# Up projection: high and low parts side by side in one tile, multiplied by the high weights in one matmul of 512 columns

## The chip, the cores and the metric

The kernel runs on one core of one Trainium2 chip. The metric is the device time of one execution in microseconds; the time before is the median of three runs.

The core has five engines, each with an instruction queue of its own that is worked off in order: PE (TensorE, matmuls; its weight loads are listed apart as PEld), DVE (VectorE), ACT (ScalarE), POOL (GpSimd) and SP (SyncE, which here only issues DMAs). They meet only at semaphores.

## The reference

One transformer block over 512 latent tokens (T) of width 2048, with a context prefix of 256 tokens, all in float32. The change is in the feed-forward part:

```python
def conv_ffn(h, w_up, cw, cb, w_down):
    u = dwconv3(h @ w_up, cw, cb)
    a, g = jnp.split(u, 2, axis=-1)
    return (a * jax.nn.silu(g)) @ w_down

# in reference(), after attention, short convolution and the output projection:
hf_l = modulate(rms_norm(x, g_ffn_norm[l]), sh_f, sc_f)
x = x + gt_f * conv_ffn(hf_l, w_up[l], ffn_conv_w[l], ffn_conv_b[l], w_down[l])
```

`h` is 512 x 2048, `w_up` is 2048 x 11008 (twice 5504: a and g), `dwconv3` a convolution of width 3 along the tokens.

## The kernel before, in words

Everything is held transposed: features on the 128 partitions, the 512 tokens along the columns. The feed-forward width of 5504 is 43 tiles of 128 (index f), each with an a part and a g part; the 2048 input features are 16 tiles (k or j).

**Float32 as two parts.** A matmul here reads operands of the type float32r. To keep float32 accuracy, every operand is split into a high part (an ACT cast to float32r) and a low part (DVE: the value minus the high part). A product is then three matmuls into the same PSUM bank: high weights x high values, high weights x low values, low weights x high values. That is `mm3` (lines 185 to 189), and so the matmuls of nearly the whole kernel stand at lines 187, 188 and 189. A tuple of two tiles, high and low, is passed as the operand.

**The inputs of the up projection.** `hf_tile` (line 931) norms and modulates tile j and splits it into `hf[j]`, two tiles of 128x512. `t_sums` (line 1075) makes from a pair of input tiles the sums and differences over the two token halves (H0, H1: columns 0 to 255 and 256 to 511) that the scheme below needs, and splits them as well: into the second half of `hf` of the even tile and into the tiles `TT`.

**The first six output tiles (uf).** The a and g parts of f = 0, 1, 2 are computed while the inputs are still being made: for k = 0 to 15, `row` (line 612) multiplies input tile k by six weight tiles into six PSUM banks. Rows 0 to 5 run in two halves of 256 columns, first all for H0, then all for H1; rows 6 to 15 (line 1155) run with 512 columns, so 18 matmuls each.

**The other 40 tiles of f.** From f = 3 on, a fast scheme for 2x2 block products is used: the blocks are the a and g part of the weights, the even and the odd input tiles, and the two token halves. It needs seven block products in place of eight, called p1, p2, p6, q5, p7, q4 and q3. Each (`product`, line 1165) has 8 input tiles of 128 and 256 columns, so 8 x 3 = 24 matmuls. Its weights, 128x1024, are split just ahead (`split4`, line 995: the high part by ACT, line 998, the low part by DVE, line 999; three buffers of each). Three PSUM banks, pa, pb and pc, are used per tile, one half of each; p6, p7 and q4 go on adding to what stands in pa, and q3 to pc. The outputs are taken out in between:

- after p1: ACT copies pa to u1 (`aside`, line 1174); after p2: DVE adds pb and u1 into the first half of cg (line 1212)
- after p6: ACT copies pa to u2; after p7: ACT copies pa to u3, and DVE makes the second half of ca from pc and u3 (line 1224)
- q4 and q3 run one tile later (`finish`, line 1177): ACT writes the first half of ca from pa with the sign changed (line 1180), DVE adds pc and u2 into the second half of cg (line 1182)

Then `acts` (line 1010) runs the convolution, the SiLU and the product of both on the full 512 columns; the result is kept (`plain`) or again turned into sums and differences (`pair_sums`, line 1035), split into high and low side by side in one tile, and stored to DRAM by POOL (line 1044), to be read again by the down projection.

**Weights.** `up_load` (line 1113) fetches five tiles of 128x1024 per f, a tile ahead, on the SP queue (line 1119); two of them get a second block added by an accumulating DMA on the POOL queue (line 1121), which must wait for the plain load. Nine buffers hold them.

**Order.** The program is written in the order of the calls, but most of it is ordered per engine by the compiler framework's scheduler, which simulates the engines' times. Only what goes through `keep` or `issue_after` has an order set by hand. So a changed instruction can change the order of others on its engine.

Of the kernel before, what the change touches and what calls it, by code (L numbers as in the profile page):

```python
# [10 lines left out]
F32 = mybir.dt.float32  # L11
# [61 lines left out]
def block_kernel(ctx, tc, xt, ctxt, ctxn, c, c_ctx, w_ada, small, w_in, w_inc, w_q, w_kv, w_out,  # L73
# [111 lines left out]
    def mm3(ps, w, x, first, last, on_top=False):  # L185
        with tc.issue_after(behind.pop()) if behind else ExitStack():
            PE.matmul(ps, w[0], x[0], start=first, stop=False, skip_group_check=on_top)  # L187
        PE.matmul(ps, w[0], x[1], start=False, stop=False, skip_group_check=on_top)  # L188
        PE.matmul(ps, w[1], x[0], start=False, stop=last, skip_group_check=on_top)  # L189


# [720 lines left out]
    def whole(raw, xs, nm, ps=None, cols=slice(0, T), ld=None, often=False):  # L912
# [162 lines left out]
    def t_sums(j):  # L1075

        e, o = xres[2 * j], xres[2 * j + 1]
        i, c = j // 2, HS[j % 2]
        if j % 2 == 0:
            for n in (1, 2, 4):  # L1080
                TT[n, i] = tuple(t2([P, T], F32R, f"T{n}{i}{z}") for z in "hl")

        def put(dst, src):
            hi, lo = dst
            A.copy(out=hi, in_=src)
            V.tensor_tensor(out=lo, in0=src, in1=hi.bitcast(F32), op=ALU.subtract)
# [3 lines left out]
        put(half_of(hf[2 * j], 1), e[:, H1])  # L1090
        V.scalar_tensor_tensor(out=o[:, H1], in0=e[:, H0], scalar=-1.0, in1=o[:, H1], op0=ALU.mult, op1=ALU.subtract)
        V.scalar_tensor_tensor(out=o[:, H0], in0=o[:, H1], scalar=-1.0, in1=o[:, H0], op0=ALU.mult, op1=ALU.subtract)
        for n, src in ((1, e[:, H0]), (2, o[:, H1]), (4, o[:, H0])):
            put(tuple(z[:, c] for z in TT[n, i]), src)

    def operand(n, j):
        if n in ("11", "3"):
            return half_of(hf[2 * j], n == "3")
        if n in ("21", "22"):
            return half_of(hf[2 * j + 1], n == "22")  # L1100
        return half_of(TT[int(n), j // 2], j % 2)

# [10 lines left out]
    def up_load(f):  # L1113
# [8 lines left out]
        return r  # L1122

    pss = [bank_of(i, f"uf{g}") for g, i in enumerate((2, 3, 4, 5, 1, 0))]
    held = [first_weights(k, k > 2) for k in range(EARLY)]
    for k in range(3, EARLY):
        hf_tile(k, H0)
    for k in range(EARLY):
        row(pss, held[k], hf[k], k, H0)
        pump(1)  # L1130
    drain()
    for k in range(EARLY):
        hf_tile(k, H1)
        row(pss, held[k], hf[k], k, H1)
        pump(1)
        if k in (3, 5):
            t_sums(k // 2 - 1)
# [9 lines left out]
    for k in range(EARLY, NK):  # L1147
        w = nxt
        if k + 1 < NK:
# [4 lines left out]
            nxt = prepare(k + 1)  # L1154
        row(pss, w, hf[k], k)
        if k % 2:
# [8 lines left out]
    def product(ps, a, n, nm, first):  # L1165

        w = split4(a, 1024, nm)
        for j in range(8):
            mm3(ps[:, :256], part(w, j), operand(n, j), first and j == 0, j == 7, on_top=not first)
        pump(1)  # L1170

    def aside(ps, nm):
        r = cp.tile([P, 256], F32, tag="uu", bufs=4, name=nm)
        A.copy(out=r, in_=ps[:, :256])
        return r

    def finish(st):
        f, a22, s4, u2, u3, pa, pc, cg, ca = st
        product(pa, a22, "4", f"u{f}q4", False)
        A.activation(ca[:, H0], pa[:, :256], AF.Identity, scale=-1.0)  # L1180
        product(pc, s4, "22", f"u{f}q3", False)
        V.tensor_tensor(out=cg[:, H1], in0=pc[:, :256], in1=u2, op=ALU.add)  # L1182
        acts(f, cg, ca)
# [15 lines left out]
    for f in range(G // 2, NF):  # L1199
# [7 lines left out]
        cg = cp.tile([P, T], F32, tag="cg", bufs=2, name=f"cg{f}")  # L1207
        ca = cp.tile([P, T], F32, tag="ca", bufs=2, name=f"ca{f}")
# [4 lines left out]
        V.tensor_tensor(out=a11, in0=a11, in1=s1, op=ALU.add)  # L1213
# [380 lines left out]
```

## Time and profile before

| | us |
|---|---|
| median of 3 runs (lowest, highest) | 2149.96 (2146.95, 2152.8) |
| the profiled execution: its own time | 2158.83 |
| its span, from the first to the last instruction | 2157.0 |
| mean granted TensorE clock in it | 0.994 |

The groups in the page name an instruction by line, engine and operation, then the tile written and the tiles read, the shapes and the count; behind the bar stand its busy time, the mean length in ns, and the idle time of the engine just before it with what ended it. A matmul's length in the timeline is not its price: matmuls overlap, and the distance from the start of one to the start of the next is what PE spends on it. `ufwk` are the weights of the first six tiles, `u18p6h` the high part of the weights of product p6 of f = 18, `u18a` its bank pa, `hf` and `T` the inputs. `d` and `dw` belong to the first part of the down projection, which uses 512 columns; `s`, `pq` and `pc` to attention and the projections ahead of it.

### The profile page before, as it was taken

The page shows a single profiled execution, that of the slowest core. Times are in us where ns is not written, and L with a number is a line of the kernel's source. Part 1 is how long each engine was busy: PE and PEld are TensorE (multiplying, and loading weights), DVE is VectorE, ACT ScalarE, POOL GpSimd, SP SyncE. Part 2 cuts the span into 40 slices and gives each one's busy share as a digit, 9 for nine tenths or more (in the row PEclk, how much of TensorE's full clock was granted, in tenths as well). Part 3 has the DMA queues.
Part 4 walks back from the last instruction along what each step waited for, and adds up shares of the span by engine and source line. Part 5 has one row for each costly group of instructions (what it writes and reads, how often), then busy time and mean ns, then how long its engine had stood idle before and what let it go on. Part 6 is the DMA issues. An engine that isn't in the chain of part 4 may idle for free.

```text
span 2157.0 us, 37744 instructions
## 1 busy us (share of the span) xinstructions
PE 2104.9 (98%) x14458; PEld 1946.7 (90%) x14458; DVE 1769.0 (82%) x2859; ACT 1047.1 (49%) x1710; POOL 188.1 (9%) x270
## 2 busy tenths in 40 slices
PE   7899999999999999999999999999999999999997
PEld 4688788888888888999999999999999889999997
DVE  7998987778886889788888788788888658888877
ACT  5533333555552237555555555555555333333445
POOL 0000000000000000111211111111111000000000
PEclk9999999999999999999999999999999999999998
DMA  9979785334559986577887877877887999877683
GB/s 335 345 275 337 270 279 176 128 126 162 177 199 348 344 278 192 159 217 201 241 232 215 240 229 220 237 231 219 241 229 218 341 335 290 254 220 236 196 247 111
DMA packets 162121, 513.89 MB, mean 238 GB/s; under 512 B 18962, under 2 KB 23314, under 8 KB 156306
## 3 DMA queue, kind: packets, MB, share of 16 engines
q1 hardware_dynamic: 133364, 418.14, 56.5%
q0 software_dynamic: 27488, 92.29, 18.3%
q8 instruction: 113, 1.85, 0.3%
q10 hardware_dynamic: 1088, 1.05, 0.1%
q14 instruction: 68, 0.56, 0.1%
HBM read 464.22 MB, written 46.14 MB: 237 GB/s over the span
## 4 chain that ended last, share of the span: by engine, by line
PE 86%; DVE 6%; DMA 5%; issue 1%; ACT 1%; SPq 0%; DVEq 0%; POOLq 0%; ACTq 0%
PE pp L187 4%; PE pp L189 4%; PE pp L188 4%; PE o L189 1%; PE o L187 1%; PE o L188 1%; DMA ada<-in_w_ada 1%; PE d L187 1%; PE d L189 1%; PE d L188 1%; PE uf L187 1%; PE uf L188 1%; PE of L187 1%; PE of L188 1%; PE of L189 1%
## 5 line engine op out<-in xcount | busy, mean ns | idle before, releaser
L1044 POOL DMA_DIRECT2D t_d<-tp x126 | 71.9, 574 | 468.3 <-DVE tp L1043 465.4
L255 DVE SCALAR_TENSOR_TENSOR ada<-ada,sv 128x1024 f32<-128x1024 f32 x68 | 82.1, 1219 | 12.1 <-DMA ada<-in_w_ada 12.0
L166 ACT CAST w_0h<-rw 128x512 fp32r<-128x512 f32 (+1 forms) x63 | 38.3, 618 | 108.3 <-PE pp L188 63.1
L1121 POOL DMA_DIRECT2D u_s<-in_w_up x80 | 70.2, 878 | 224.4 <-DMA u_s<-in_w_up 131.5
L233 DVE SCALAR_TENSOR_TENSOR ada<-ada,sv 128x1024 f32<-128x1024 f32 x64 | 77.5, 1217 | 4.4 <-DMA ada<-in_w_ada 3.9
L522 DVE SCALAR_TENSOR_TENSOR ada<-ada,svc 128x1024 f32<-128x1024 f32 x64 | 76.0, 1220 | 2.3 <-DMA ada<-in_w_ada 2.3
L785 POOL TENSOR_TENSOR gr<-gr,half 128x8 f32<-128x8 f32 x4 | 10.1, 2524 | 628.7 <-DVE gr L784 536.8
L1042 ACT CAST tp<-a 128x256 fp32r<-128x256 f32 x90 | 34.7, 405 | 60.5 <-DMA t_d<-tp 54.1
L167 DVE TENSOR_TENSOR w_0l<-rw,w_0h 128x512 fp32r<-128x512 f32 (+1 forms) x63 | 42.6, 681 | 22.3 <-ACT w_0h L166 22.3
L255 DVE SCALAR_TENSOR_TENSOR ra<-ra,sv 128x1024 f32<-128x1024 f32 x44 | 52.5, 1217 | 1.1 <-DMA ra<-in_w_ada 1.1
L1213 DVE TENSOR_TENSOR u<-u,u_s 128x1024 f32<-128x1024 f32 x40 | 48.8, 1219 | 0.7 <-DMA u_s<-in_w_up 0.7
L1214 DVE TENSOR_TENSOR u<-u,u 128x1024 f32<-128x1024 f32 x40 | 48.7, 1218 | 0.0
L1043 DVE TENSOR_TENSOR tp<-a,tp 128x256 fp32r<-128x256 f32 x90 | 36.2, 418 | 12.3 <-ACT tp L1042 12.3
L756 ACT CAST pth<-t 128x384 fp32r<-128x384 f32 x64 | 28.6, 485 | 26.4 <-PE t L753 26.4
L1042 ACT CAST tp<-ts 128x256 fp32r<-128x256 f32 x36 | 14.6, 407 | 43.5 <-DMA t_d<-tp 41.1
L533 DVE TENSOR_TENSOR acc<-acc,pp 128x512 f32<-128x512 f32 x50 | 34.0, 680 | 2.1 <-PE pp L189 2.1
L757 DVE TENSOR_TENSOR ptl<-t,pth 128x384 fp32r<-128x384 f32 x64 | 33.2, 549 | 2.7 <-ACT pth L756 2.7
L737 DVE TENSOR_REDUCE mn<-s 128x1 f32<-128x768 f32 x32 | 30.4, 952 | 4.8 <-PE s L726 4.6
L1043 DVE TENSOR_TENSOR tp<-ts,tp 128x256 fp32r<-128x256 f32 x36 | 15.2, 421 | 23.3 <-ACT tp L1042 23.3
L1005 ACT ACTIVATE g<-cg,sm 128x512 f32<-128x512 f32 x40 | 32.5, 813 | 0.5 <-DVE cg L1182 0.5
L1005 ACT ACTIVATE a<-ca,sm 128x512 f32<-128x512 f32 x40 | 32.1, 803 | 0.0
L1013 ACT ACTIVATE g<-g 128x512 f32<-128x512 f32 x43 | 27.2, 632 | 6.4 <-DVE g L1007 6.4
(15967 smaller groups left out, 9398.2 us busy)
## 6 DMA issues: line engine op xcount, KB each, us to landing
ada<-in_w_ada SPq DMA_DIRECT2D x196, 512.0 KB, 6.0
u<-in_w_up SPq DMA_DIRECT2D x120, 512.0 KB, 8.2
w<-t_d SPq DMA_DIRECT2D x161, 256.0 KB, 5.2
u_s<-in_w_up SPq DMA_DIRECT2D x80, 512.0 KB, 4.3
u_s<-in_w_up POOLq DMA_DIRECT2D x80, 512.0 KB, 8.9
t_d<-tp POOLq DMA_DIRECT2D x126, 256.0 KB, 4.9
v<-in_w_dnw SPq DMA_DIRECT2D x72, 384.0 KB, 5.4
ra<-in_w_ada SPq DMA_DIRECT2D x22, 1024.0 KB, 4.9
```

Source lines behind the costliest of these rows:

```text
L187: PE.matmul(ps, w[0], x[0], start=first, stop=False, skip_group_check=on_top)
L188: PE.matmul(ps, w[0], x[1], start=False, stop=False, skip_group_check=on_top)
L189: PE.matmul(ps, w[1], x[0], start=False, stop=last, skip_group_check=on_top)
L233: V.scalar_tensor_tensor(out=r, in0=r, scalar=1.0, in1=vec[:, i * 1024:(i + 1) * 1024], op0=ALU.mult, op1=ALU.mult, accum_out=col[:, i:i + 1])
L255: keep(V.scalar_tensor_tensor(out=r, in0=r, scalar=1.0, in1=svs[i], op0=ALU.mult, op1=ALU.mult, accum_out=lc[:, t % 4:t % 4 + 1] if i else ...
L522: keep(V.scalar_tensor_tensor(out=raw[q], in0=raw[q], scalar=1.0, in1=svc[:, q * 1024:(q + 1) * 1024], op0=ALU.mult, op1=ALU.mult, accum_o ...
L1005: A.activation(u, src, AF.Identity, bias=s("fb", m), scale=s("fw", 86 + m))
L1042: A.copy(out=z[:, :256], in_=src)
L1043: V.tensor_tensor(out=z[:, 256:], in0=src, in1=z[:, :256].bitcast(F32), op=ALU.subtract)
L1044: G_.dma_start(t_d[p, OPS.index(n)], z.bitcast(F32))
L1121: G_.dma_start(r[-1], src[more], accum_op=ALU.add)
L1213: V.tensor_tensor(out=a11, in0=a11, in1=s1, op=ALU.add)
```

## The change

High and low part of one operand of 256 columns now lie side by side in one tile of 128x512: `hf[j, h]` for the token half h of input tile j, and `TT[n, j]`. In `product`, one matmul of 512 columns multiplies the whole tile by the high weights, and a second of 256 columns multiplies the high half by the low weights (`mm2`). The bank then holds two sums side by side, which have to be added: the outputs are taken out of PSUM with 512 columns, and GpSimd adds the two halves (`halves`). The rows of the first six tiles use the same inputs, so they run in halves of 256 columns throughout (`up_row`, with `mm3`). The copies u1, u3 and the new u4 share two buffers of 128x512, u2 has one, ca has one in place of two.

```diff
+    def mm2(ps, w, x, first, last, on_top=False):
+        n = x.shape[1] // 2
+        with tc.issue_after(behind.pop()) if behind else ExitStack():
+            PE.matmul(ps[:, :2 * n], w[0], x, start=first, stop=False, skip_group_check=on_top)
+        PE.matmul(ps[:, :n], w[1], x[:, :n], start=False, stop=last, skip_group_check=on_top)
...
+    def side_by_side(z, src):
+        n = T // 2
+        A.copy(out=z[:, :n], in_=src)
+        return V.tensor_tensor(out=z[:, n:], in0=src, in1=z[:, :n].bitcast(F32), op=ALU.subtract)
...
     def hf_tile(j, cols=slice(0, T)):
-        if j not in hf:
-            hf[j] = tuple(t2([P, T], F32R, f"hf{j}{z}") for z in "hl")
...
-        hi, lo = (z[:, cols] for z in hf[j])
-        A.copy(out=hi, in_=xr)
-        ins = V.tensor_tensor(out=lo, in0=xr, in1=hi.bitcast(F32), op=ALU.subtract)
+        for h in range(2):
+            if cols in (HS[h], slice(0, T)):
+                hf[j, h] = t2([P, T], F32R, f"hf{j}{h}")
+                ins = side_by_side(hf[j, h], xres[j][:, HS[h]])
...
+    def up_row(w, k, hs=(0, 1)):
+        for g in range(G):
+            for h in hs:
+                mm3(pss[g][:, HS[h]], w[g], (hf[k, h][:, :256], hf[k, h][:, 256:]), k == 0 and h == 0, k == NK - 1 and h == 1)
...
-        row(pss, w, hf[k], k)
+        up_row(w, k)
...
-            mm3(ps[:, :256], part(w, j), operand(n, j), first and j == 0, j == 7, on_top=not first)
+            mm2(ps, part(w, j), operand(n, j), first and j == 0, j == 7, on_top=not first)
...
+    def parts(nm):
+        two = nm.endswith("2")
+        return cp.tile([P, 512], F32, tag="u2" if two else "uu", bufs=1 if two else 2, name=nm)
+
     def aside(ps, nm):
-        r = cp.tile([P, 256], F32, tag="uu", bufs=4, name=nm)
-        A.copy(out=r, in_=ps[:, :256])
+        r = parts(nm)
+        A.copy(out=r, in_=ps)
         return r
+
+    def halves(dst, r):
+        G_.tensor_tensor(out=dst, in0=r[:, :256], in1=r[:, 256:], op=ALU.add)
...
-        A.activation(ca[:, H0], pa[:, :256], AF.Identity, scale=-1.0)
+        u4 = parts(f"u{f}4")
+        A.activation(u4, pa, AF.Identity, scale=-1.0)
+        halves(ca[:, H0], u4)
         product(pc, s4, "22", f"u{f}q3", False)
-        V.tensor_tensor(out=cg[:, H1], in0=pc[:, :256], in1=u2, op=ALU.add)
+        V.tensor_tensor(out=u2, in0=pc, in1=u2, op=ALU.add)
+        halves(cg[:, H1], u2)
         acts(f, cg, ca)
...
-        V.tensor_tensor(out=cg[:, H0], in0=pb[:, :256], in1=u1, op=ALU.add)
+        V.tensor_tensor(out=u1, in0=pb, in1=u1, op=ALU.add)
+        halves(cg[:, H0], u1)
...
-        V.scalar_tensor_tensor(out=ca[:, H1], in0=pc[:, :256], scalar=-1.0, in1=u3, op0=ALU.mult, op1=ALU.subtract)
+        ca = cp.tile([P, T], F32, tag="ca", bufs=1, name=f"ca{f}")
+        V.scalar_tensor_tensor(out=u3, in0=pc, scalar=-1.0, in1=u3, op0=ALU.mult, op1=ALU.subtract)
+        halves(ca[:, H1], u3)
```

The same number of columns is streamed through PE per product: 8 x 3 x 256 before, 8 x (512 + 256) after. `t_sums` writes through `side_by_side` and allocates one `TT` tile per input pair and sum; its arithmetic is the same.

More of the change, by code (lines that the diff above doesn't have):

```diff
@@ L1077, in t_sums @@
         e, o = xres[2 * j], xres[2 * j + 1]
[L1078 to L1086, printed above, removed]
         V.tensor_tensor(out=e[:, H0], in0=e[:, H0], in1=e[:, H1], op=ALU.subtract)
         V.tensor_tensor(out=e[:, H1], in0=o[:, H1], in1=e[:, H1], op=ALU.subtract)
-        put(half_of(hf[2 * j], 1), e[:, H1])
+        side_by_side(hf[2 * j, 1], e[:, H1])
         V.scalar_tensor_tensor(out=o[:, H1], in0=e[:, H0], scalar=-1.0, in1=o[:, H1], op0=ALU.mult, op1=ALU.subtract)
@@ L1128, in block_kernel @@
     for k in range(EARLY):
-        row(pss, held[k], hf[k], k, H0)
+        up_row(held[k], k, (0,))
         pump(1)
@@ L1133, in block_kernel @@
         hf_tile(k, H1)
-        row(pss, held[k], hf[k], k, H1)
+        up_row(held[k], k, (1,))
         pump(1)
@@ L1207, in block_kernel @@
         cg = cp.tile([P, T], F32, tag="cg", bufs=2, name=f"cg{f}")
-        ca = cp.tile([P, T], F32, tag="ca", bufs=2, name=f"ca{f}")
         product(pa, a11, "11", f"u{f}p1", True)
```

9 lines of the change are left out of this document (5 added, 4 removed).

## The prediction

> **What bounds the kernel now.** I read the page's totals first, then busy time by stretches, then the timeline inside one stretch. This is the page's line of engine totals, and two stretches: one inside the tiled up projection and one in the down projection behind it.
>
> ```profile
> span 2157.0 us, 37744 instructions
> ...
> PE 2104.9 (98%) x14458; PEld 1946.7 (90%) x14458; DVE 1769.0 (82%) x2859; ACT 1047.1 (49%) x1710; POOL 188.1 (9%) x270
> ...
> 1100.00:1200.00 100.00, 100.00 (x836) 100.00 (x835) 82.39 (x112) 56.80 (x88) 18.75 (x28) 1.00 0.79 224
> 1700.00:1780.00 80.00, 80.00 (x386) 66.72 (x385) 46.11 (x95) 27.92 (x40) 4.96 (x8) 1.00 0.96 341
> ```
>
> The columns of a stretch are its length, then busy time on PE, weight loads, DVE, ACT and POOL, the granted clock, the DMA share and GB/s. In both stretches PE never rests and the clock is full, so only the spacing of the matmuls sets the time. In the up projection the weight loads fill the whole stretch too; in the down projection, whose matmuls have 512 columns, they fill 66.72 of 80 us. A busy PE is not yet a PE at its peak, so the spacing itself has to be read, from the timeline (start, length, engine, line). The first two rows are the start of the same product of two neighbouring tiles of the up projection, 168 matmuls apart (7 products of 24); the next two are 264 matmuls of 512 columns apart (11 rows of 24).
>
> ```profile
> 1204.14 0.28 PE L187 MATMUL u19b<-hf1h,u19p2h 128*128 128x256 f32 x1
> ...
> 1224.30 0.28 PE L187 MATMUL u20b<-hf1h,u20p2h 128*128 128x256 f32 x1
> ```
>
> ```profile
> 1703.24 0.39 PE L187 MATMUL d<-yl2h,dw02h 128*128 128x512 f32 x1
> ...
> 1764.58 0.40 PE L187 MATMUL d<-yl6h,dw16h 128*128 128x512 f32 x1
> ```
>
> The tiled up projection lasts from its first matmul to the first piece of the chain of waits that is not its own:
>
> ```profile
> 884.46 0.29 PE L187 MATMUL u3a<-hf0h,u3p1h 128*128 128x256 f32 x1
> ```
>
> ```profile
> 1685.02 0.14 PE u42a L188
> 1685.18 1.05 ACT dw00h L998
> ```
>
> 20.16 us / 168 = 120.0 ns for 256 columns; 61.34 us / 264 = 232.3 ns for 512. Two matmuls of 256 cost 240.0 ns, one of 512 costs 232.3: putting two side by side is worth 7.7 ns if each keeps its steady spacing.
>
> **What the change saves on PE.** A triple (high x high, high x low, low x high) is now 3 x 120.0 = 360.0 ns and becomes one matmul of 512 and one of 256. The columns streamed stay at 768; one matmul and one weight load go. By the steady spacings the pair costs 352.3 ns. But no steady stream of 512 and 256 in alternation exists in this trace. The nearest rows are places where a 512 is followed by 256s; the first and last of 39 such places in the stretch from 300 to 760 us:
>
> ```profile
> 410.45 0.40 PE L189 MATMUL pq<-qa3h,wq01l 128*128 128x512 f32 x1
> 410.68 0.29 PE L187 MATMUL pc<-hc,wc_0h 128*128 128x256 f32 x1
> 410.80 0.28 PE L188 MATMUL pc<-hc,wc_0h 128*128 128x256 f32 x1
> ...
> 608.28 0.39 PE L726 MATMUL s<-krll,qst 128*128 128x512 f32 x1
> 608.51 0.28 PE L722 MATMUL s<-kcx,q31h 128*128 128x256 f32 x1
> 608.62 0.28 PE L723 MATMUL s<-kcx,q31h 128*128 128x256 f32 x1
> ```
>
> Here 512 plus 256 take 350 and 340 ns; over the 39 places the mean is 347.5. So a 256 right behind a 512 is a little cheaper than 120.0, which fits the weight loads: they fill the stretch of 256s and leave room in that of 512s. The two ends are 352.3 and 347.5; I take the middle, 350.0, because the alternation is between the two kinds of row. That saves 10.0 ns per triple (7.7 to 12.5). There are 40 tiles x 7 products x 8 = 2240 triples: **-22.4 us** (-17.2 to -28.0).
>
> **The price in the rows ahead.** The first six output tiles are computed row by row. Its rows 6 to 15 used 18 matmuls of 512 columns each; as high and low of one half now share a tile, they become 36 of 256. Each row goes from 18 x 232.3 = 4.18 us to 36 x 120.0 = 4.32 us, and PE is the engine that lasts there as well (50.00 of 50 us busy in the next row): 10 x 0.14 = **+1.4 us**. The early rows 0 to 5 already run in halves; nothing changes for PE.
>
> ```profile
> 840.00:890.00 50.00, 50.00 (x251) 42.09 (x250) 42.50 (x82) 32.44 (x58) 2.55 (x3) 1.00 0.51 121
> ```
>
> **The other engines.** Each output now leaves PSUM as 512 columns, and a GpSimd add folds the halves: per tile three DVE instructions and four ACT instructions grow from 256 to 512 columns, and POOL gets four adds of 128x256. The prices, from the page's groups and from two tiles (min/median/max):
>
> ```profile
> L1043 DVE TENSOR_TENSOR tp<-a,tp 128x256 fp32r<-128x256 f32 x90 | 36.2, 418 | 12.3 <-ACT tp L1042 12.3
> ...
> L533 DVE TENSOR_TENSOR acc<-acc,pp 128x512 f32<-128x512 f32 x50 | 34.0, 680 | 2.1 <-PE pp L189 2.1
> ```
>
> ```profile
> L1174 ACT COPY u<-u18a x3: 360/364/365, 1185.1 to 1202.5; 128x256 f32<-128x256 f32 x3
> ```
>
> ```profile
> L1316 ACT COPY c<-d x16: 579/588/649, 1727.6 to 1770.9; 128x512 f32<-128x512 f32 x16
> ```
>
> DVE: 82.39 per 100 us is 16.6 us of a 20.16 us period. Three times 680 - 418 ns add 0.8 us: 17.4 us, in a new period of 20.16 - 56 x 0.010 = 19.6 us, so 89%. ACT: 56.80 per 100 is 11.5 us, plus 4 x 0.22 = 0.9: 12.4 of 19.6. Neither becomes the bound by itself, and both stay beside PE: cost nothing. The cover is that weights are split up to two products ahead. Were DVE to fill its period, every further us of DVE per tile would cost 40 us.
>
> POOL: no add of this size is in the trace. The bounds are DVE's own 0.42 us for 256 columns and the only add that POOL runs here, a narrow one at 2.52 us, in the group below. Four of them are 1.7 to 10.1 us in a period of 19.6, beside 3.8 us of DMA issues (18.75 per 100): room enough. I take 0.8 us each, nearer to the row of equal size, since the other is 8 columns wide and mostly start-up. An add that ended early could gain nothing, as nothing but the later activations waits for it.
>
> ```profile
> L785 POOL TENSOR_TENSOR gr<-gr,half 128x8 f32<-128x8 f32 x4 | 10.1, 2524 | 628.7 <-DVE gr L784 536.8
> ```
>
> **The new waits.** POOL takes its work in order: behind each add stand the accumulating weight loads (L1121) and the stores of the pair sums (L1044). The adds wait for DVE, the weight loads for the plain loads under them. The tightest buffer is u2, of which there is one: it is free only after the add behind product q3, and the ACT copy of product p6 needs it, and that copy must be done before p7 accumulates into the same bank. Rows of one tile:
>
> ```profile
> 1192.82 0.42 DVE L1182 TENSOR_TENSOR cg<-u17c,u 128x256 f32<-128x256 f32 x1 [0.29 <-PE u17c L189]
> ```
>
> ```profile
> 1196.54 0.36 ACT L1174 COPY u<-u18a 128x256 f32<-128x256 f32 x1
> ```
>
> ```profile
> 1198.62 0.28 PE L187 MATMUL u18a<-hf0h,u18p7h 128*128 128x256 f32 x1
> ```
>
> After the change the DVE add ends at about 1193.5, the copy of 0.59 us must begin by about 1198.0, so POOL has 4.5 us for its 0.8 us. Unless it stands behind a long wait, nothing is late. The last tile's fold adds about 1 us to a chain that ends in stores which are read again some 80 us later: nothing.
>
> Sum: -22.4 + 1.4 = -21.0 us. The profiled execution took 2158.8 us (span 2157.0 and 1.8 around it), the median of the runs is 2149.96, 8.9 us lower; the same matmuls stand in both, so the difference carries over: 2137.8 in a profiled execution, **2129 us** by the median. About 0.3% (6.4 us) is what a measurement of this kernel can tell from no change.
>
> **Rivals.**
>
> Little saved on PE. If the weight load behind the short matmul is late for the long one each time, by up to the 7.7 ns, the pair costs what three matmuls did or a little less; with the +1.4 us that is 2146 to 2151. Against it stand both spacings above, for it only that none is of a real alternation. The Trainium skill has a rule that points this way: its page "TensorE: Matmul & The Clock Gate", section "Back-to-back issue gap", gives columns/2.4 ns plus a fixed 2.5 ns for each warm matmul, so dropping one of three would be worth 2.5 ns, 2240 x 2.5 = 5.6 us, and the time about 2146 (an estimate from that page). This trace disagrees as far as it goes: two 256s exceed one 512 by 7.7 ns, not 2.5.
>
> DVE becomes the bound. Its adds read two SBUF operands, and POOL now does the same beside it. DVE has 19.6 - 17.4 = 2.2 us free per tile; if each POOL add held DVE up for more than 0.55 us, DVE would set the period. At 0.8 us held up in full the period is 17.4 + 3.2 = 20.6, over 20.16: 40 x 0.44 + 1.4 = +19, 2169. At 0.6 it is 19.8, and 40 x 0.36 - 1.4 = 13 are gained: 2137. For it: DVE's additions of two SBUF operands, 1219 ns each in the row below, have had no wide POOL add beside them.
>
> ```profile
> L1213 DVE TENSOR_TENSOR u<-u,u_s 128x1024 f32<-128x1024 f32 x40 | 48.8, 1219 | 0.7 <-DMA u_s<-in_w_up 0.7
> ```
>
> Against it: 2.2 us is much for a port, and the four adds are short. The Trainium skill's "GPSIMD Engine Reference", section "Key points", says that GpSimd shares its SBUF interfaces with VectorE and contends with DVE instructions that have two SBUF inputs; no run here shows it yet.
>
> The POOL queue holds PE up; this ends slower. POOL waits long for the plain loads; first the line of the waits (in total, times, longest), then the group of its issues:
>
> ```profile
> POOL u_s L1121 <- DMA u_s<-in_w_up: 119.7, 57, 5.8
> ```
>
> ```profile
> L1121 POOL DMA_DIRECT2D u_s<-in_w_up x80 | 70.2, 878 | 224.4 <-DMA u_s<-in_w_up 131.5
> ```
>
> The waits are 2.1 us on average and 5.8 at most. A fold that stands behind such a wait comes 2.1 + 0.9 (the issue) + 0.8 = 3.8 us after DVE, inside the 4.5; behind a longest one 7.5, which stalls p7 by 3 us. It decides once the wait passes 2.8 us. If every tile met it: 40 x 3 - 21 = +99, 2249; with one tile in three, 40 - 21 = +19, 2169. Against it: the order on POOL is chosen anew, and PE did not wait at all in these stretches.
>
> **Chances.** Forecast (PE bound, pair near 350 ns) 0.68; little saved 0.10; DVE near its limit 0.09 (0.04 still faster, 0.05 slower); POOL queue 0.13, slower. Faster 0.72, same 0.10, slower 0.18. The forecast's own range: -28.0 + 1.4 gives 2123, -17.2 + 1.4 gives 2134; with 4 us of scatter in a median of three, 2119 to 2138. The full range goes up over the DVE case at 2137 and the little-saved case to 2152 and leaves most of the slower cases out: 2119 to 2152.
>
> **What would show it.** Right: in the up projection two matmuls per triple, the same product of neighbouring tiles 19.6 us apart (19.46 to 19.73), PE busy in full, DVE near 89%, POOL adds under 1 us, 17 us or more off between 884 and 1685, rows 6 to 15 at 4.32 us. Wrong: PE idle in that stretch with a DVE low part or an ACT copy as the releaser; two-operand DVE instructions much longer than 1219 ns while POOL adds run; ACT copies into u2 that wait for POOL; or a period above 20 us with PE full, which would mean that the alternation costs more than either stream.

## The result, and the profile after

The changed kernel takes 2262.51 us (median of 4 runs, 2261.52 to 2264.13), the kernel before in the same session 2151.38 (2146.95 to 2159.54): a ratio of 1.051, 95% interval 1.048 to 1.0545. It is 111 us slower; 2129 was forecast. The profiled execution took 2262.49 us, 103.7 more than that of before, and nearly all of it lies in one stage: from the first matmul of u3p1 to the last of u42q3 pass 919.2 us (881.32 to 1800.52), where it had been 810.3 (884.46 to 1694.76). What lies ahead of the stage is 3.1 us shorter, what lies behind it 2.0.

The totals of the page after, then the same stretch of the up projection that was shown of before (columns: length, busy PE, PEld, DVE, ACT, POOL, granted clock, DMA share, GB/s):

```profile
span 2260.7 us, 33900 instructions
...
PE 2124.5 (94%) x12398; PEld 1851.4 (82%) x12398; DVE 1849.8 (82%) x2869; ACT 1074.1 (48%) x1720; POOL 380.7 (17%) x430
```

```profile
1100.00:1200.00 100.00, 90.00 (x481) 76.94 (x480) 78.91 (x95) 50.05 (x73) 34.38 (x38) 0.95 0.70 200
```

2060 matmuls are gone, yet PE has more busy time and idles for 10 of 100 us; the granted clock is 0.95. No other engine is full: DVE and ACT do less per 100 us than before (82.39 and 56.80). So no engine's work sets the period; waits do. But the matmuls themselves do what was forecast where nothing disturbs them. From the timeline of PE:

```profile
1207.79 0.39 PE L196 MATMUL u17a<-T,u17q4h 128*128 128x512 f32 x1
1208.02 0.28 PE L197 MATMUL u17a<-T,u17q4l 128*128 128x256 f32 x1
1208.13 0.39 PE L196 MATMUL u17a<-T,u17q4h 128*128 128x512 f32 x1
...
1209.88 0.40 PE L196 MATMUL u17a<-T,u17q4h 128*128 128x512 f32 x1
```

Six pairs in 2.09 us; over the undisturbed pairs of the stage 230.7 ns from a 512 to its 256 and 120.1 ns back, 350.8 ns. The waits come on top. Start-to-start distances above these add up to 130.1 us in the stage (1.3 before). PE is idle for 87.2 us of the stage by the profile. A part of the rest is a slower PE behind some of the waits; the timeline of one, then a stretch that covers most of the slow rows (same columns as above):

```profile
1203.56 0.39 PE L197 MATMUL u18b<-hf,u18p2l 128*128 128x256 f32 x1 [0.76 <-DVE u18p2l L1013]
...
1204.51 0.41 PE L197 MATMUL u18b<-hf,u18p2l 128*128 128x256 f32 x1
1204.73 0.63 PE L196 MATMUL u18b<-hf,u18p2h 128*128 128x512 f32 x1
1205.15 0.41 PE L197 MATMUL u18b<-hf,u18p2l 128*128 128x256 f32 x1
1205.37 0.63 PE L196 MATMUL u18b<-hf,u18p2h 128*128 128x512 f32 x1
```

```profile
1204.20:1207.60 3.40, 3.40 (x12) 2.92 (x12) 3.40 (x4) 1.44 (x3) 0.00 (x0) 0.50 0.34 65
```

A pair takes 0.64 us here where it takes 0.35 a few rows later, and the granted clock in these 3.4 us is 0.50. Over the whole stage it is 0.97, against 1.00 before: 3% of 919.2 us, so about 28 us of the excess (an estimate). The waits of PE are each put down to a weight part or to a copy out of PSUM; these are the longest of each kind in the view of the waits (in total, times, longest):

```profile
PE u22b L196 <- ACT u22p2h L1012: 3.6, 1, 3.6
PE u42a L196 <- ACT u L1189: 3.3, 1, 3.3
```

Added up by kind: ACT's cast of p2 30.1 us, ACT's copy out of pa 24.0, DVE's low parts of p1 19.5 and of p2 11.1. Most of it starts at ACT, which is half idle; the low parts of p2 start on DVE right behind their casts. Those of p1 do not: their casts have ended earlier, and most of these parts are themselves long, up to 2.5 us in place of 1.22, while a fold runs on POOL. One of them on DVE, the fold on POOL, and PE behind it:

```profile
1334.08 2.50 DVE L1013 TENSOR_TENSOR u24p1l<-u,u24p1h 128x1024 fp32r<-128x1024 f32 x1
```

```profile
1334.47 1.01 POOL L1194 TENSOR_TENSOR cg<-u 128x256 f32<-128x256 f32 x1
```

```profile
1336.63 0.39 PE L197 MATMUL u24a<-hf,u24p1l 128*128 128x256 f32 x1 [1.02 <-DVE u24p1l L1013]
```

Counted wait by wait, the extra length of these parts explains at most 14 of the 87.2 us (an estimate). For the rest one asks what ACT waits for, in the stage; first before, then after:

```profile
ACT tp L1042 <- DMA t_d<-tp: 95.2, 62, 2.9
```

```profile
ACT tp L1056 <- DMA t_d<-tp: 152.2, 47, 6.0
ACT u L1200 <- POOL ca L1194: 66.9, 27, 3.5
ACT g L1019 <- POOL cg L1194: 41.6, 34, 2.4
```

The `t_d` lines are the cast of a pair sum (in `pair_sums`, L1042 before and L1056 after). Its tile is free only when an earlier store to `t_d` has landed: the pool has 58 tiles, `hf` takes 32 and `TT` 24, so two pair sums can be under way. The wait existed before, in 62 short pieces behind which PE did not wait. Now single waits are longer, up to 6.0 us, while the casts of the weights and the copies stand behind it on ACT. The two other lines are new, and are waits for the folds on POOL. The page's chain of the work that ended last, which follows each wait back to what ended it, puts the stores first of all it lists by line (shares of the span); before, they are not in that list:

```profile
DMA t_d<-tp 12%; DMA u_s<-in_w_up 4%; POOL ca L1194 4%; PE pp L189 3%; PE pp L187 3%; PE pp L188 3%; DMA ada<-in_w_ada 2%; PE o L189 1%; PE o L187 1%; PE o L188 1%; PE d L187 1%; PE d L188 1%; PE d L189 1%; PE uf L187 1%; PE uf L189 1%
```

The folds themselves and the stores, in the page's groups and its list of DMA issues (last figure: us from issue to landing; before 4.9):

```profile
L1194 POOL TENSOR_TENSOR ca<-u 128x256 f32<-128x256 f32 x80 | 131.3, 1642 | 26.6 <-DVE u L1247 20.9
L1058 POOL DMA_DIRECT2D t_d<-tp x126 | 76.5, 641 | 311.0 <-DVE tp L1057 301.4
...
L1194 POOL TENSOR_TENSOR cg<-u 128x256 f32<-128x256 f32 x80 | 86.1, 1076 | 14.2 <-DVE u L1233 13.2
```

```profile
t_d<-tp POOLq DMA_DIRECT2D x126, 256.0 KB, 7.5
```

### The profile page after: what moved, and what is told of

Read it like the earlier page. It is cut to its first block, busy times and chain, and to the rows that moved or that the text cites. A ratio compares the mean times of both kernels' runs of the same rounds, so it can differ in the third digit from the quotient of the medians.

```text
span 2260.7 us, 33900 instructions
## 1 busy us (share of the span) xinstructions
PE 2124.5 (94%) x12398; PEld 1851.4 (82%) x12398; DVE 1849.8 (82%) x2869; ACT 1074.1 (48%) x1720; POOL 380.7 (17%) x430
## 4 chain that ended last, share of the span: by engine, by line
PE 56%; DMA 20%; DVE 10%; POOL 6%; issue 5%; ACT 3%; POOLq 0%; SPq 0%; ACTq 0%; DVEq 0%
DMA t_d<-tp 12%; DMA u_s<-in_w_up 4%; POOL ca L1194 4%; PE pp L189 3%; PE pp L187 3%; PE pp L188 3%; DMA ada<-in_w_ada 2%; PE o L189 1%; PE o L187 1%; PE o L188 1%; PE d L187 1%; PE d L188 1%; PE d L189 1%; PE uf L187 1%; PE uf L189 1%
## 5 line engine op out<-in xcount | busy, mean ns | idle before, releaser
L1194 POOL TENSOR_TENSOR ca<-u 128x256 f32<-128x256 f32 x80 | 131.3, 1642 | 26.6 <-DVE u L1247 20.9
L1058 POOL DMA_DIRECT2D t_d<-tp x126 | 76.5, 641 | 311.0 <-DVE tp L1057 301.4
L1194 POOL TENSOR_TENSOR cg<-u 128x256 f32<-128x256 f32 x80 | 86.1, 1076 | 14.2 <-DVE u L1233 13.2
L1056 ACT CAST tp<-ts 128x256 fp32r<-128x256 f32 x36 | 14.6, 405 | 136.3 <-DMA t_d<-tp 134.7
L1057 DVE TENSOR_TENSOR tp<-a,tp 128x256 fp32r<-128x256 f32 x90 | 51.3, 599 | 19.9 <-ACT tp L1056 19.8
L263 DVE SCALAR_TENSOR_TENSOR ra<-ra,sv 128x1024 f32<-128x1024 f32 x44 | 52.5, 1219 | 1.0 <-DMA ra<-in_w_ada 1.0
L1236 DVE TENSOR_TENSOR u<-u,u 128x1024 f32<-128x1024 f32 x40 | 48.7, 1219 | 0.0
L1056 ACT CAST tp<-a 128x256 fp32r<-128x256 f32 x90 | 33.3, 406 | 22.5 <-DMA t_d<-tp 17.5
L971 POOL DMA_DIRECT2D x_d<-x x18 | 10.0, 554 | 160.9 <-DVE x L969 137.1
```

Of the source, the lines that this page charges most:

```text
L263: keep(V.scalar_tensor_tensor(out=r, in0=r, scalar=1.0, in1=svs[i], op0=ALU.mult, op1=ALU.mult, accum_out=lc[:, t % 4:t % 4 + 1] if i else ...
L1057: V.tensor_tensor(out=z[:, 256:], in0=src, in1=z[:, :256].bitcast(F32), op=ALU.subtract)
L1058: G_.dma_start(t_d[p, OPS.index(n)], z.bitcast(F32))
L1194: G_.tensor_tensor(out=dst, in0=r[:, :256], in1=r[:, 256:], op=ALU.add)
L1236: V.tensor_tensor(out=a12, in0=a12, in1=a11, op=ALU.add)
```

## The experiments

Each run is compared with runs of the kernel before on the same chip; "stall" is the excess of PE's start-to-start distances in the stage, worked out as above (before 1.3, after 130.1).

### First set: the folds, POOL and the layout

Three theories at first: the folds' place in POOL's queue; POOL's additions slowing DVE; the new layout and its longer instructions. The folds on DVE:

```diff
-        G_.tensor_tensor(out=dst, in0=r[:, :256], in1=r[:, 256:], op=ALU.add)
+        V.tensor_tensor(out=dst, in0=r[:, :256], in1=r[:, 256:], op=ALU.add)
```

> The changed kernel with the four folds of a tile on DVE in place of POOL; nothing else. Theory Q (queue): POOL's folds come late because they stand behind other work in POOL's queue, ACT waits for them at the head of its own queue and the weight casts behind it are late. Theory P (port): a POOL add and a DVE instruction with two SBUF operands hold each other up, so folds and low parts both become long. Without any add on POOL both vanish: low parts back at 1.22 us each (1.34 on average now), products at 2.81 us one after the other, period 19.65 us, time 2130 to 2137. Theory D (DVE is simply too full): DVE now has 17.4 + 4 x 0.34 = 18.8 us of work in 19.65; if it has no room left for its own order, PE stalls stay, DVE shows no idle time and the time stays above 2160.

Measured 2307.81, ratio 1.072 (1.070 to 1.074): slower still, with no addition on POOL. Stall 174.3. That the folds on POOL are the whole cost fell here. DVE is not full either: it is busy for 74.79 us of the stretch from 1100 to 1200.

The reverse: the kernel before, with four additions of the folds' size per tile on POOL, whose results nothing uses (they read what DVE or ACT has just written and write into a tile that is otherwise unused):

```diff
+    def unused_add(src):
+        G_.tensor_tensor(out=rl[:, :256], in0=src, in1=rl[:, 256:], op=ALU.add)
```

> The kernel before, plus four POOL adds of 128x256 per tile that read the four finished halves of cg and ca and write to a tile that nobody reads; so no instruction waits for an add, except that they stand in POOL's queue and read SBUF. Theory P: the adds alone lengthen DVE's low parts (1.22 us) as in the changed kernel, by about 34 us over the stage, and the adds themselves range from 0.72 to over 3 us; if that is what holds PE up, the time rises by 30 us or more, to above 2180. Theory Q: nobody waits, so the time stays within 8 us of before (2143 to 2159), even if adds and low parts are long.

Measured 2225.74, 1.034 (1.032 to 1.035); stall 77.4. Additions whose results nobody uses cost 74 us.

The third gives u4 a buffer of its own, so that ACT's copy does not wait for the fold ahead:

```diff
-        u4 = parts(f"u{f}4")
+        u4 = rl
```

> The changed kernel with a buffer of its own for u4, the copy that ACT makes after q4 (a tile that is free in this stage); u1 and u3 keep the two others. Folds stay on POOL. Theory Q: ACT's 67 us of waiting for the fold of u3 before it can write u4 go, and the casts behind it come in time; the time falls by 50 us or more, to below 2212; the waits of the activation for the fold into cg (42 us) stay. Theory P: the folds are as long as now and hold DVE up as now; the time falls by less than 20 us.

Measured 2264.47, 1.0526 (1.0503 to 1.0548): no gain. In its waits the line of 66.9 us for POOL's `ca` is gone, and the stores' line (142.1 us, 49 times) is nearly what it was. So ACT's second largest wait was worth nothing.

The fourth keeps the side-by-side tiles and the rows in halves but takes the three matmuls of 256 columns into half a bank, without folds:

```diff
-            mm2(ps, part(w, j), operand(n, j), ...)
+            mm3(ps[:, :256], part(w, j), (operand(n, j)[:, :256], operand(n, j)[:, 256:]), ...)
```

> The layout alone: high and low side by side, rows 0 to 15 in halves, but three matmuls of 256 columns into half a bank as before, no fold, the outputs taken out as before. All theories: rows 6 to 15 at 4.27 us (4.18 before), products at 2.88 us; the time within 8 us of before, 2147 to 2157. Anything above 2165 would mean that the layout itself costs.

Measured 2144.19 (10 runs), 0.9968 (0.9954 to 0.9982): a little faster than before, the only version here that is. The layout costs nothing; the cost comes with the wide bank and its folds. One stretch of e2, then one of e4:

```profile
1100.00:1200.00 100.00, 94.31 (x771) 92.03 (x770) 82.95 (x103) 52.60 (x81) 37.75 (x41) 1.00 0.76 212
```

```profile
1100.00:1200.00 100.00, 100.00 (x845) 100.00 (x844) 84.11 (x114) 58.44 (x90) 19.23 (x29) 1.00 0.82 238
```

### Second set: the stores of the pair sums

What e1 and e2 share is neither a fold on POOL nor a wider copy. In e1's trace one can follow a long wait through three timelines, POOL, ACT and PE:

```profile
1427.65 0.86 POOL L1126 DMA_DIRECT2D u_s<-in_w_up  x1 [3.46 <-DMA u_s<-in_w_up]
1428.21 1.42 POOL L1058 DMA_DIRECT2D t_d<-tp  x2
1439.76 0.54 POOL L1058 DMA_DIRECT2D t_d<-tp  x1 [10.13 <-DVE tp L1057]
```

```profile
1438.61 0.40 ACT L1056 CAST tp<-ts 128x256 fp32r<-128x256 f32 x1 [6.34 <-DMA t_d<-tp]
1438.92 0.81 ACT L1019 ACTIVATE g<-cg,sm 128x512 f32<-128x512 f32 x1
1439.63 0.80 ACT L1019 ACTIVATE a<-ca,sm 128x512 f32<-128x512 f32 x1
1440.34 0.56 ACT L1189 COPY u<-u26a 128x512 f32<-128x512 f32 x1
```

```profile
1436.37 0.28 PE L197 MATMUL u27a<-hf,u27p1l 128*128 128x256 f32 x1
1440.95 0.65 PE L196 MATMUL u26a<-hf,u26p7h 128*128 128x512 f32 x1 [4.30 <-ACT u L1189]
```

Two stores are issued right behind an accumulating load of 512 KB. Some 10 us later the cast that needs their tile starts, behind it in ACT's queue comes the copy of u26's p6, and p7 waits 4.30 us for that copy. So the new theory: the stores land too late, ACT stands at the head of its queue for a free tile, and PE pays. Four edits: a third tile for the pair sums; the stores on SP; both folds on DVE and stores on SP; and the unused additions of e2 with the stores on SP.

```diff
-            z = t2([P, T], F32R, f"tp{p}{n}")
+            puts[0] += 1
+            z = rl.bitcast(F32R) if puts[0] % 3 == 0 else t2([P, T], F32R, f"tp{p}{n}")
```

> The changed kernel; every third pair sum is split into a tile that is free in this stage, so that three instead of two stores of pair sums can be under way. Nothing else. Theory S (stores): ACT's cast of a pair sum stands at the head of ACT's queue until an earlier store has landed (152 us in the changed kernel, up to 6.0 each; 95 before, up to 2.9), and the copies out of PSUM and the weight casts behind it are late. Then ACT's waits for t_d fall below 60 us, PE idles less and the time falls by 50 us or more, to below 2212. Theory P (port: adds and two-operand DVE instructions hold each other up): the folds stay as long as they are and the time falls by less than 20 us.

Measured 2208.64, 1.026 (1.0235 to 1.028): one more tile of 256 KB gives back 54 us. Its ACT waits for stores fall from 152.2 us to 67.3, while the waits for folds stay:

```profile
ACT u L1202 <- POOL ca L1196: 63.9, 30, 3.5
ACT g L1019 <- POOL cg L1196: 50.3, 35, 3.0
ACT tp L1058 <- DMA t_d<-tp: 43.4, 10, 7.4
ACT rl L1058 <- DMA t_d<-rl: 23.9, 6, 4.9
```

```diff
-            G_.dma_start(t_d[p, OPS.index(n)], z.bitcast(F32))
+            SP.dma_start(t_d[p, OPS.index(n)], z.bitcast(F32))
```

> The changed kernel with the stores of the pair sums issued by SP instead of POOL; folds and accumulating weight loads stay on POOL. A store then stands neither behind a fold nor behind an accumulating load of 512 KB (9.0 us to landing). Theory S: landing falls from 7.5 to under 5 us, ACT's waits for t_d nearly go, the time falls by 50 us or more, to below 2212, and if the stores were all of it to 2130 to 2140. Theory P: less than 20 us, above 2240.

> Folds on DVE, stores of the pair sums on SP: POOL keeps the accumulating loads alone. With folds on DVE and stores on POOL the time was 2307.8, ACT waited 170 us for t_d and the landing took 7.9 us. Theory S: that was the stores' doing; the time falls below 2150, to 2130 to 2140 if DVE, with 18.8 us of work in a period of 19.65, keeps up. If DVE is simply too full, it stays above 2200 with DVE over 93% busy.

> The kernel before with the four unused POOL adds per tile (2225.7, so 74 us slower than before without anyone waiting for them) and the stores of the pair sums on SP. Theory S: the adds cost that much only because stores and accumulating loads queue behind them; with the stores on SP at least half of the 74 us goes, below 2189. Theory P: the adds cost because they lengthen DVE's instructions (25 us over the low parts); less than 25 us goes, above 2200.

Measured: f2 2225.49, 1.032 (1.028 to 1.0355); f3 2205.91, 1.024 (1.022 to 1.027), 102 us under e1; f4 2155.42 (10 runs), 1.001 (0.9997 to 1.0022). The last makes the clearest pair of the study. e2 and f4 differ only in the queue of the stores. All four unused additions per tile stay on POOL, and nearly the whole 74 us are gone, with PE full again:

```profile
1100.00:1200.00 100.00, 100.00 (x841) 100.00 (x840) 89.79 (x113) 56.67 (x88) 34.17 (x30) 1.00 0.80 228
```

So what POOL's additions cost is what they do to the stores behind them. In f2 and f3 a part of the loss stays: on SP the stores still take 6.5 and 9.2 us to land (f4: 4.7). Why they take longer there is not shown.

### Third set: order in the program, and the matmul itself

The pair sums' pieces were put further apart in the program, to let weight casts pass between them:

```diff
             put(...)
+            yield
```

> The changed kernel with one pair sum split and stored after every second product in place of every product, so that the seven of a pair fill all 14 products of two tiles; folds and stores stay on POOL. Theory S (ACT stands at its cast of a pair sum until an earlier store has landed): a store now has some 11 us to land, ACT's waits for t_d fall from 152 to under 40 us and the time by 60 us or more, to below 2200; a rest stays where ACT waits for the folds themselves (67 and 42 us). Theory O (order: each edit gives another order on the engines, and most of them are bad): no such fall, the time anywhere from 2190 to 2300 with the waits for t_d hardly fewer.

> The same spreading with the folds on DVE, stores on POOL (2307.8 without the spreading). Theory S: neither stores nor folds hold ACT up any longer; 2128 to 2145, period 19.65 us, PE busy in full. If DVE is too full with 18.8 us in 19.65, or the order is bad by itself: above 2170, with copies out of PSUM or low parts as PE's releasers and ACT's waits for t_d below 40 us all the same.

> Folds on DVE, spreading, and every third pair sum in a tile that is free in this stage, so three stores can be under way. Theory S: if some waits for t_d are left with the spreading alone, they go here; within 5 us of the kernel with the spreading alone if none were left, otherwise faster by what they cost.

Measured: h1 2259.13, 1.051; h2 2309.26, 1.0736; each the time of its version without the edit. It missed as an edit: the scheduler put the engines' work into nearly the same order (ACT's wait for stores in h1: 152.1 us, 48 times). h3 adds the third tile to h2: 2223.63, 1.034 (1.032 to 1.036), 86 us less for a tile.

h4 takes the one matmul of h2 apart again, into two of 256 columns in the two halves of the bank:

```diff
-            PE.matmul(ps[:, :2 * n], w[0], x, ...)
+            PE.matmul(ps[:, :n], w[0], x[:, :n], ...)
+        PE.matmul(ps[:, n:2 * n], w[0], x[:, n:], ...)
```

> The kernel with spreading and folds on DVE, but the matmul of 512 columns undone into two of 256 into the two halves of the bank: three matmuls per triple, everything else the same. It prices the matmul by itself. From the changed kernel's own spacing (230.7 + 120.1 = 350.8 ns against 360): if PE sets the time in both, this one is slower by 2240 x 9 ns = 20 us (15 to 25). If other engines set it, the difference is under 8 us.

Measured 2301.73, 1.070 (1.068 to 1.072), 7.5 us under h2: with the saving on PE taken out, nothing is lost. Where ACT's waits set the time, the saving doesn't show.

### Fourth set: the one buffer of u2

Before, ACT copies into u2 right behind the weight cast of the next p1 (in all 36 tiles counted, f = 5 to 40). After has the two activations of the tile ahead, which wait for a fold, in between (33 of 36); e1 has a cast of a pair sum there as well in 16 of 36. The single buffer of u2, now 512 columns, is busy till its fold is done. A second one:

```diff
+        if two:
+            turns[0] += 1
+            if turns[0] % 2 == 0:
+                return rl
```

> The changed kernel with a second buffer for u2 (every second one in a tile that is free in this stage). In the kernel before, ACT's copy of u2 stands right behind the weight cast of the next p1; in the changed kernel it stands behind a cast of a pair sum, which waits for a store, and behind the activations of the tile before, which wait for a fold, and p7 waits for the copy. Theory U (one u2 buffer: its copy can't be placed before the fold of the tile before has freed it, so it is queued behind the other work that the fold releases): with two buffers the copy stands in its old place; PE's waits for copies go; the time falls by 50 us or more, to below 2212; a rest from the folds on POOL may stay. Theory S (the stores alone, wherever the copy stands): less than 20 us.

> The same with the folds on DVE (2307.8 with one u2 buffer). Theory U: no copy out of PSUM is late, nothing waits for POOL; 2128 to 2150, products at 2.81 us one after the other, PE busy in full, stores still 7 to 8 us to landing with some waits of ACT that reach nobody. Theory S: ACT still stands at its casts of pair sums for 100 us or more and PE with it; above 2230.

> Folds on DVE, two u2 buffers, but the matmul of 512 columns undone into two of 256 into the two halves of the bank. It prices the matmul by itself once nothing else holds PE up: by the spacings of the changed kernel (350.8 against 360 ns) it is slower than the kernel with the 512 columns by 20 us (15 to 25). If the difference is under 8 us, PE does not set the time in one of them.

> Folds on DVE, two u2 buffers and the stores of the pair sums on SP. If stores still cost something with two u2 buffers, it is faster than that kernel by it; by theory U within 6 us of it.

Measured: j1 (folds on POOL) 2251.73, 1.047 (1.043 to 1.050), 11 us under after; j2 (folds on DVE) 2225.89, 1.035 (1.032 to 1.038), 82 under e1; j5, j2 with three matmuls, 2224.28, no difference; j6, j2 with the stores on SP, 2199.89, 1.022 (1.018 to 1.025). The copy into u2 is back in its old place (33 of 36 tiles in j1, all in j2). But PE's waits for ACT's copies, which theory U let go, stay: 30 us in j1 (24 after), 55 in j2 (64 in e1). The place of the copy is worth much with folds on DVE, little with those on POOL. None of them comes near the time before, and ACT still waits 106.8 us for stores in j2.

### Fifth set: without the wait for the stores

Last, after and j2 with stores that read a constant tile, so that no pair sum is stored and none waits for a landing. The down projection then works on other numbers:

```diff
-            G_.dma_start(t_d[p, OPS.index(n)], z.bitcast(F32))
+            G_.dma_start(t_d[p, OPS.index(n)], sm[:, :T])
```

> The changed kernel with every store of a pair sum reading a constant tile in place of the tile just split: the same DMAs of the same size on the same queue, but no cast of ACT has to wait for a store to land (the stored pair sums are not the computed ones, so the down projection works on other numbers). One u2 buffer, folds on POOL. Theory S (ACT stands at a cast until a store has landed, and PE starves behind it): the waits of ACT for t_d are gone, and the time falls by 60 us or more, to below 2200. Theory F (the folds on POOL: ACT waits 67 us for the fold of u3 and 42 us for that of cg): what stays above 2131 is theirs; if they are the main part, it stays above 2210.

> Folds on DVE, two u2 buffers, and the stores reading the constant tile: nothing is left for ACT to wait long for (the stored pair sums are again not the computed ones). Theory S: PE sets the time; products at 2.81 us throughout, PE idle under 5 us in the stage, 2127 to 2137, so about 20 us below the kernel before: the saving of the matmul of 512 columns, as the spacings give it. If DVE is too full with 18.8 us in 19.65, PE still idles with low parts as its releasers and the time is above 2145.

Measured: k1 2187.88, 1.016 (1.014 to 1.017); k2 2184.89, 1.014 (1.012 to 1.016). By the total, neither beats before. But the edit did more than was meant, as POOL's rows of `t_d` show (min/median/max ns, first and last start):

```profile
L1058 POOL DMA_DIRECT2D t_d<-sm x126: 539/542/725, 19.2 to 187.3; - x126
```

With nothing to wait for, all 126 stores went out in the kernel's first 190 us, which are bound by loads; these are two stretches of k1, then one of after:

```profile
0.00:100.00 100.00, 69.48 (x213) 46.41 (x214) 59.85 (x113) 48.70 (x85) 34.42 (x67) 0.91 1.00 396
100.00:200.00 100.00, 86.82 (x351) 67.90 (x350) 78.66 (x146) 27.45 (x47) 34.02 (x63) 0.95 1.02 414
```

```profile
0.00:100.00 100.00, 80.66 (x279) 54.99 (x280) 83.77 (x164) 59.96 (x105) 0.20 (x4) 1.00 0.93 349
```

So the stage begins at 928.50 in k1, 47 us later than in after, for a reason that has nothing to do with the question. The stage itself is what tells: 796.6 us in k1 and 792.6 in k2, against 810.3 before and 919.2 after. Stall 8.1 and 3.1. A stretch of each, k1 first:

```profile
1300.00:1400.00 100.00, 100.00 (x571) 87.60 (x570) 93.03 (x117) 62.94 (x91) 40.26 (x30) 1.00 0.71 187
```

```profile
1300.00:1400.00 100.00, 100.00 (x572) 87.64 (x572) 95.03 (x136) 63.03 (x92) 8.52 (x10) 1.00 0.72 189
```

PE is full at full clock. A tile has 112 matmuls, so the period is 112/571 x 100 = 19.6 us, the forecast's. k1 keeps the folds on POOL, the one u2 and the wider copies. It does not keep the order on ACT: the copy into u2 is back behind the cast of p1 in 34 of 36 tiles. j1 has that order with the waits, and gained 11 us only. The edit took out the wait, the stores' traffic in the stage and their issues on POOL together; f1 and h3, which keep traffic and issues, got back 54 and 86 us by easing the wait alone.

## Why the prediction was wrong

**What held.** The pair costs 350.8 ns (350.0 forecast), the rows 6 to 15 take 4.27 us each (4.32). Without the wait for the stores, 13.7 of the forecast 22.4 us are there in k1's stage, with the folds on POOL, and 17.7 in k2's, with ACT at 63% as worked out. DVE is at 93% in k1 (89 forecast). A fold on POOL takes 0.72 us where nothing disturbs it (0.8 forecast), but 1.36 on average. Against e4 less is left: its 256s stand 118.7 ns apart, three make 356.0, and 2240 x 5.2 ns = 12 us is what the wide matmul is worth beside that spacing; the stages differ by 801.4 - 792.6 = 8.8. The rival "little saved" is thereby out. By the formula of the Trainium skill's "TensorE: Matmul & The Clock Gate", section "Back-to-back issue gap", which the page gives for an isolated matmul, dropping one is worth 2.5 ns (an estimate from that page). The trace has 9.2 against before (360.0 - 350.8) and 5.2 against e4.

**The step that failed** is "Neither becomes the bound by itself, and both stay beside PE: cost nothing", with the one behind it, "nothing is late". ACT's price was taken as busy time in a period, 12.4 of 19.6 us. But ACT is an ordered queue with a wait in it that the work of other tiles decides: the cast of a pair sum for the landing of a store. The page of before showed it (L1042 waited 54.1 us for t_d in one group, 41.1 in another); it stood in no sum, as PE was idle for 1.0 us only. The prediction even named what makes the stores late, "behind each add stand the accumulating weight loads (L1121) and the stores of the pair sums (L1044)", and then priced how late an add may come, not how late a store may.

ACT's waits for stores went from 95.2 to 152.2 us, and PE's stall from 1.3 to 130. The long single waits tell, not their sum: f4 has 107.8 us of them and loses next to nothing. Over 4 us there is none before, none in e4 and one in f4, but 20 in after, 27 in e1, 17 in e2 and 9 in j6 (92.8 us in all). So there was slack of some us behind each wait, and the change used it up. The later stores are shown to do that, and the place of the copy into u2 in part; ACT's wider copies were not tried by themselves.

**Why the stores land later.** Two things can be counted in the traces by pairing each store with the end of its low part on DVE and with the last accumulating load on POOL. Before, a store is issued 0.40 us after its data are ready (mean of 126), and 18 of 126 are issued within 2 us of the issue of an accumulating load ahead. e4 has 0.42 and 18. After, it is 1.46 us, with 37 over 1.5 us, and 38 stand that close behind a load. j2, without folds on POOL, has 0.37 and 41; e2, with nothing but additions on POOL, 1.30 and 2. So the counts point to two ways to be late: behind POOL's additions (e2), and close behind a load (j2); after has both. f4 tests the first; no run tests the second by itself. The order of loads and stores on POOL is no different in j2 than before: 50 of its 126 stores follow a load in both. Only the time between them shrank. From data ready to landing pass 5.3 us before (median), 5.5 in e4, 6.5 in j2, 7.3 in e2, 8.1 after and 8.6 in e1; the stalls are 1.3, 1.3, 91, 77, 130 and 174. With a third tile it matters less: f1 has 10.0 us and a stall of 69. That a load comes closer to the store because ACT, waiting, frees the weight buffers later, so that the wait feeds itself, fits this but was only argued. What sets it off in j2, where POOL does no additions, is open.

**The rivals.** "The POOL queue holds PE up" came nearest: it had the side, the queue and the accumulating loads, at 0.13. But it had the folds behind the loads and u2 as the wait; k1 has the folds and one u2 and a stall of 8.1, and e3 took away ACT's largest wait for a fold for nothing. The prediction had missed that wait ("nothing but the later activations waits for it"): ACT's copy after q4 stands behind a fold for 66.9 us in all. It is the stores, behind folds and, by the counts, behind loads. Its range of 2169 to 2249 was still too low by 13.5; the lower clock alone is some 28. "DVE becomes the bound" did not happen: 78.91 busy in 100 after. POOL's additions do lengthen DVE's low parts (below), by 34 us in all in after and 30 in f4, and f4 is as fast as before. So by itself this costs nothing; behind a late ACT it holds PE up too, by the 14 us above at most.

**What the test said.** "PE idle with a DVE low part or an ACT copy as the releaser" was named as a sign of being wrong, and is what the profile shows. So was the next, two-operand DVE instructions much longer than 1219 ns while POOL adds run. The first names the last link; the releaser's own wait has to be read next.

**What is left.** No version beats e4 (0.9968), which leaves the matmul alone, and none with the wide matmul is as fast as before in total. Whether the wide matmul would gain with still more tiles for the pair sums was not tried beyond the third of f1 and h3.

## What to carry to other kernels

An engine that is half idle is not free: before a copy is widened on it, list what its queue waits for at the head, and ask how long a single one of these waits may grow before someone behind it is late. A wait that costs nothing today can be a buffer count near its limit. And when a releaser is named in a wait, follow it one engine further, until the answer is a DMA or a full engine; then test it with one more buffer or another queue, not by moving the newest instruction.

## What the runs showed of the hardware

POOL's fold of 128x256 has no fixed price: 0.72 us in one place, over 3 in another. Its timeline in after, with DVE's beside it:

```profile
1328.09 3.25 POOL L1194 TENSOR_TENSOR ca<-u 128x256 f32<-128x256 f32 x1
1331.31 0.72 POOL L1194 TENSOR_TENSOR cg<-u 128x256 f32<-128x256 f32 x1
```

```profile
1327.71 1.22 DVE L1013 TENSOR_TENSOR u23p6l<-u,u23p6h 128x1024 fp32r<-128x1024 f32 x1
1328.85 0.75 DVE L1057 TENSOR_TENSOR tp<-a,tp 128x256 fp32r<-128x256 f32 x2
1329.52 1.22 DVE L1013 TENSOR_TENSOR u23q5l<-u_s,u23q5h 128x1024 fp32r<-128x1024 f32 x1
1330.66 0.68 DVE L1203 TENSOR_TENSOR u<-u22c,u 128x512 f32<-128x512 f32 x1
```

The long addition lasts as long as DVE runs instructions with two operands in SBUF back to back, and ends 0.7 us after one starts that reads PSUM (u22c); the second has DVE idle beside it. Of the 160 folds 43 take up to 0.76 us, and 40 of these have no DVE instruction with two operands in SBUF beside them. Turned round, DVE's low parts of 128x1024 take 1.22 us and up to 3.3 where they meet an addition (33 of 280 over 1.4 us). The Trainium skill's "GPSIMD Engine Reference", section "Key points", says that the two share their SBUF interfaces; the trace agrees, and puts up to 4.0 us on an addition of 0.72.

Undisturbed matmuls of 256 columns have more than one spacing. They stand 118.7 ns apart in e4 and 118.8 in j5, against 120.0 before; over 6720 of them that is the 9 us by which e4's stage is shorter. It is not the side-by-side tiles: e2 and f4, with the tiles of before, have 118.9 and 119.2, and f4 has stretches of both kinds, 836 matmuls in the 100 us from 1300 and 845 in those from 1500. What sets it is open.
